# Layer A's input branches of quarters 2 to 4 by seven half-size block products, token-major

## The chip, the cores and the metric

The kernel runs on one core of a Trainium2 chip. The metric is the device time of one execution in microseconds. The page and the trace come from one profiled execution. TensorE is PE in the rows (its weight loads PEld), VectorE is DVE, ScalarE ACT, GpSimd POOL, and SP issues all the DMAs of this kernel in one queue.

## What is computed

A trunk of two layers on 2048 tokens of width 1024, in float32. Layer A is a gated MLP with mixing among the tokens of a chunk of 128; layer B is dilated attention over three groups of heads that share one K/V. The change is in layer A:

```python
def gmlp_layer(x, c, ada_w, ada_b, norm_g, w_in, sgu_g, w_s, b_s, w_out):
    h = rms_norm(x, norm_g) * (1 + scale) + shift        # 2048 x 1024
    u, v, z = jnp.split(h @ w_in, 3, axis=-1)             # three branches, 2048 x 2048 each
    u = jax.nn.gelu(u)
    v = rms_norm(jax.nn.gelu(v), sgu_g)
    mixed = jnp.einsum('gts,bcsge->bctge', jnp.tril(w_s), v) + b_s.T[...]   # 8 groups of 256
    y = u * mixed * jax.nn.silu(z)
    return x + gate * (y @ w_out)
```

## The kernel before

The tokens go through in four quarters of 512 (Q = 0 to 3 in the code, quarters 1 to 4 here), four tiles of 128 each. For each quarter TensorE does layer A (the branches v, u, z, then the output product o), then the projections for layer B (K/V and three q blocks and a z block). The attention of quarter Q-1 (`attend_local`) runs between the matmuls of quarter Q's layer A, and the rest of the attention in the last quarter's projections and in `finish`.

Each float32 product is made of three matmuls (`mm3`): the operands are split into a high part (ScalarE, L242) and a low part (L246; VectorE, with every fourth on GpSimd once `share` is 4), and high x high, high x low and low x high are summed in a bank of PSUM. A matmul has 512 columns. Weights come through SP as raw tiles of 128x512 (six buffers), and stand as split tiles in eight buffers.

In layer A, `dense` makes v by token: a block of 512 outputs for four tiles of tokens is 96 matmuls, and four blocks make the branch. `v_evac` takes gelu and the sum of squares. `dense_f` makes u and z by feature: 256 outputs for 512 tokens, eight calls of 48 matmuls for each. `mix` forms the spatial product by feature (L637, four matmuls of 128 columns, each two passes in the trace) and adds the bias at L639; the results `mt` are multiplied by gelu(u) at L650 and by silu(z) at L662, and split into `yh` and `yl` (L664, L665), which the product o (`dense(yT, a_w_out, ...)`) reads.

In layer B, `dense_s` makes 1024 outputs for 512 tokens by seven products of half the size in each direction instead of eight: seven times 24 matmuls, where the plain form has 192. It reads seven combinations of blocks of the input (`make_ops`: 11, 12, 22, s1 to s4) and combinations of weight blocks that `combine_weights` forms once (four subtractions on GpSimd per step, four steps per block of 1024 columns) and stores in HBM (`wt`). Sums of products are made on VectorE at L361 into tiles `st`. The next product on the same two banks can begin only when they have been emptied.

What runs between matmuls is a list of generators, `fillers`. Each `tick` adds `rate` to a counter, and `fill` takes one step of the next generator for each whole number, in turn. So `rate` sets how thickly attention, the next quarter's input (`make_hA`), the modulation vectors (`ada_acc`) and the weight combinations are spread over the matmuls. `drain` runs the list to its end. The engines' queues are in order; a scheduler that merges the streams decides the order within each, and most buffers are pools whose waits it sets.

The functions that the change touches, and what calls them, with the line numbers of the profile:

## Time and profile before

| what | value |
|---|---|
| median of 3 runs | 3120.85 us (3115.68 to 3136.62) |
| profiled execution | 3119.88 us; its span 3118.1 us |
| mean granted TensorE clock | 0.986 |
| TensorE busy | 2991.9 us, 96% |
| VectorE, ScalarE, GpSimd busy | 1943.9 us, 1629.5 us, 1207.0 us |
| DMA | 547.81 MB, 176 GB/s in the mean |
| layer A of quarter 1: v, u, z, o begin | 28.4, 142.6, 248.6, 355.7 us |
| layer A of quarters 2, 3, 4: v begins | 688.3, 1358.7, 2036.0 us |
| o begins in quarters 2, 3, 4 | 1020.9, 1708.1, 2391.8 us |
| layer B's projections begin in quarters 1 to 4 | 447.5, 1116.6, 1803.7, 2482.6 us |
| last output stage begins | 2834.6 us |

The stages are cut where the first matmul of each begins. A row of the table by stage gives the busy time of each engine in such a stretch. A row of a group gives busy time and the mean duration of one instruction in ns, then the idle time of the engine before it and what ended that. Busy time of TensorE says little by itself, since its matmuls overlap; the distance from start to start is its pace.

### The profile page before, as it was taken

What the parts mean: (1) busy time and instruction counts of PE and PEld (TensorE: products, weight loads), DVE (VectorE), ACT (ScalarE), POOL (GpSimd) and SP (SyncE); (2) the same over time, 40 slices, a digit from 0 to 9 for tenths busy, and PEclk for the clock granted to TensorE, in tenths of its full rate; (3) what the DMA queues carried; (4) which work ended last, traced back from release to release, by engine and by line L of the source; (5) the groups of instructions that cost most, each with busy time, mean ns of one, the idle gap of its engine ahead of it and who ended that gap; (6) DMA issues with size and microseconds to landing.
All of it is one profiled execution on the core that took longest, in us unless ns stands there. A gap on an engine that the chain in (4) does not pass through costs nothing.

```text
span 3118.1 us, 45175 instructions
## 1 busy us (share of the span) xinstructions
PE 2991.9 (96%) x14928; PEld 2500.8 (80%) x14928; DVE 1943.9 (62%) x3286; ACT 1629.5 (52%) x3325; POOL 1207.0 (39%) x1376
## 2 busy tenths in 40 slices
PE   6998999999999999999999999999999999999999
PEld 5887778778888777788887878778888788877787
DVE  6765457673567376765677276756676476767861
ACT  4422335557556245566466265566465357767540
POOL 4134335551124235644245145634344252244332
PEclk9999999999999999999999999999999999999999
DMA  7877647673433367663433366743433356678742
GB/s 232 272 248 250 227 153 222 220 234 120 149 105 105 93 193 232 206 207 115 140 102 98 98 201 205 241 163 106 133 108 102 122 182 210 223 241 283 236 154 95
DMA packets 341182, 547.81 MB, mean 176 GB/s; under 512 B 35818, under 2 KB 135372, under 8 KB 340948
## 3 DMA queue, kind: packets, MB, share of 16 engines
q1 hardware_dynamic: 340948, 544.93, 54.4%
q8 instruction: 118, 1.93, 0.3%
q14 instruction: 116, 0.95, 0.1%
HBM read 439.28 MB, written 105.52 MB: 175 GB/s over the span
## 4 chain that ended last, share of the span: by engine, by line
PE 62%; POOL 8%; DMA 8%; issue 6%; DVE 4%; ACT 3%; SPq 1%; POOLq 0%; DVEq 0%; ACTq 0%
PE pd_o L264 11%; PE pd_v L264 8%; PE pd_kv L264 7%; PE po L969 3%; PE pd_u L301 3%; PE pd_u L299 3%; PE pd_u L300 3%; PE pd_z L299 2%; PE pd_z L301 2%; PE pd_z L300 2%; DMA qt<-qd 1%; PE pm L637 1%; PE pq L857 1%; DMA cw<-in_b_w_in_dram 1%; PE pf L1145 1%
## 5 line engine op out<-in xcount | busy, mean ns | idle before, releaser
L264 PE MATMUL pd_v<-w_v,hAh 128*128 128x512 f32 x1024 | 328.8, 402 | 1.2 <-ACT hAh L425 1.2
L264 PE MATMUL pd_o<-w_o,yh 128*128 128x512 f32 x1024 | 320.9, 394 | 2.1 <-ACT z L660 1.8
L264 PE MATMUL pd_kv<-w_kv,hkh 128*128 128x512 f32 x768 | 245.0, 398 | 3.4 <-DVE w_kv L246 3.2
L264 PEld LDWEIGHTS pd_o<-w_o,yh 128*128 128x128 f32 x1024 | 193.7, 190 | 43.6 <-ACT z L660 2.3
L264 PEld LDWEIGHTS pd_v<-w_v,hAh 128*128 128x128 f32 x1024 | 190.4, 192 | 40.3 <-issue 1.7
L299 PE MATMUL pd_z<-hAh,w_z 128*128 128x512 f32 x512 | 207.6, 405 | 12.8 <-ACT z L660 12.7
L299 PE MATMUL pd_u<-hAh,w_u 128*128 128x512 f32 x512 | 206.4, 403 | 0.0
L908 ACT ACTIVATE pr<-pr,stat,rt 128x256 f32<-128x256 f32 (+1 forms) x320 | 177.4, 556 | 53.4 <-DVE stat L902 31.4
L264 PE MATMUL pd_v<-w_v,hAl 128*128 128x512 f32 x512 | 203.0, 397 | 0.0
L301 PE MATMUL pd_z<-hAh,w_z 128*128 128x512 f32 x512 | 202.3, 395 | 0.0
L300 PE MATMUL pd_z<-hAl,w_z 128*128 128x512 f32 x512 | 201.6, 394 | 0.0
L264 PE MATMUL pd_o<-w_o,yl 128*128 128x512 f32 x512 | 200.8, 392 | 0.0
L301 PE MATMUL pd_u<-hAh,w_u 128*128 128x512 f32 x512 | 200.4, 391 | 0.0
L300 PE MATMUL pd_u<-hAl,w_u 128*128 128x512 f32 x512 | 199.7, 390 | 0.0
L264 PEld LDWEIGHTS pd_kv<-w_kv,hkh 128*128 128x128 f32 x768 | 145.7, 191 | 38.2 <-DVE w_kv L246 7.8
L242 ACT ACTIVATE w_o<-raw_o 128x512 fp32r<-128x512 f32 x128 | 80.0, 629 | 176.4 <-PE pd_o L264 128.7
L242 ACT ACTIVATE w_z<-raw_z 128x512 fp32r<-128x512 f32 x128 | 77.5, 626 | 178.2 <-DMA raw_z<-in_a_w_in_dram 74.9
L242 ACT ACTIVATE w_u<-raw_u 128x512 fp32r<-128x512 f32 x128 | 79.2, 630 | 169.7 <-PE pd_u L301 101.8
L969 PEld LDWEIGHTS po<-kv,pT 128*128 128x128 f32 x1200 | 148.0, 192 | 16.0 <-POOL pT L943 6.6
L969 PE MATMUL po<-kv,pT 128*128 128x128 f32 x1200 | 151.9, 277 | 7.3 <-POOL pT L943 6.2
L264 PE MATMUL pd_kv<-w_kv,hkl 128*128 128x512 f32 x384 | 152.5, 397 | 0.0
L246 DVE TENSOR_TENSOR w_o<-raw_o,w_o 128x512 fp32r<-128x512 f32 x96 | 68.6, 720 | 132.0 <-ACT w_o L242 131.4
(686 smaller groups left out, 7998.4 us busy)
## 6 DMA issues: line engine op xcount, KB each, us to landing
raw_q<-in_b_w_in_dram SPq DMA_DIRECT2D x144, 256.0 KB, 3.5
raw_v<-in_a_w_in_dram SPq DMA_DIRECT2D x128, 256.0 KB, 4.1
raw_u<-in_a_w_in_dram SPq DMA_DIRECT2D x128, 256.0 KB, 2.7
raw_z<-in_a_w_in_dram SPq DMA_DIRECT2D x128, 256.0 KB, 3.1
raw_o<-in_a_w_out_dram SPq DMA_DIRECT2D x128, 256.0 KB, 2.7
qt<-qd SPq DMA_DIRECT2D x96, 260.0 KB, 3.3
raw_kv<-in_w_kv_dram SPq DMA_DIRECT2D x96, 256.0 KB, 3.0
od<-ot SPq DMA_DIRECT2D x96, 256.0 KB, 3.0
```

The lines of the kernel that those rows point to most:

```text
L242: nc.scalar.activation(hi, src, AF.Copy)
L246: e.tensor_tensor(lo, src, hi.bitcast(F32), ALU.subtract)
L264: last_mm[0] = nc.tensor.matmul(pt, a, u[:, w, :], start=f, stop=e, skip_group_check=more)
L299: nc.tensor.matmul(pts[i], wh, hh[:, k, :], start=k == 0, stop=False)
L300: nc.tensor.matmul(pts[i], wh, hl[:, k, :], start=False, stop=False)
L301: nc.tensor.matmul(pts[i], wl, hh[:, k, :], start=False, stop=k == KT - 1)
L637: nc.tensor.matmul(pm[:, t * P:(t + 1) * P], m[e // 8][:, t, (e % 8) * P:(e % 8 + 1) * P], wst[:, e // 2, :], start=True, stop=True)
L857: nc.tensor.transpose(pq[:, h * P:(h + 1) * P], u["qt"][:, h * P:(h + 1) * P], ident)
L908: nc.scalar.activation(pr[:, i, :], pr[:, i, :], AF.Exp, bias=mneg[:, i:i + 1], scale=u["rt"][:, h:h + 1], accum_out=lsum[:, i:i + 1])
L969: nc.tensor.matmul(po[:, h * P:(h + 1) * P], u["pT"][h // hp][:, h % hp, j, :], u["kv"][:, j, kh, 1, :], start=j == 0, stop=j == nk - 1)
L1145: nc.tensor.matmul(pt, yb[:, 0, k, :], wh[:, k, :], start=k == 0, stop=False)
```

## The change

In quarters 2 to 4 the branches v, u and z are made by `dense_s`, two blocks of 1024 outputs each, and all by token. `make_hA` now forms the seven input combinations instead of one pair of high and low parts. `combine_weights` forms the weight combinations of six more blocks, 24 steps more; a step is now loaded, subtracted and stored in three different turns, in buffers of attention that are idle in the first quarter (`rooms`). `layer_A_in` scales v by VectorE between the products of u (`plan`, `jobs`), mixes by token (32 matmuls of 256 columns, L805), gates the result in place with gelu(u) and then silu(z), and turns it to features with 64 transposes per quarter (`to_features`): half of them after the fourth product of z's second block, half at the end. Quarter 1 keeps its form. The rates of the fillers change, and attention is no longer bound to end with z: it runs on into o.

```diff
+    blocks = {f"b{b}": (b_w_in, b * D) for b in range(4)}
+    for j in range(2):
+        blocks.update({f"u{j}": (a_w_in, j * D), f"v{j}": (a_w_in, AW + j * D),
+                       f"z{j}": (a_w_in, 2 * AW + j * D)})
...
     def combine_weights():
...
+        for i in range(len(todo) + 2):
+            if 0 <= i - 2:
+                store(i - 2)
+            yield
+            if i < len(todo):
+                load(i)
+            yield
+            for h in range(2):
+                if 0 <= i - 1 < len(todo):
+                    combine(i - 1, h)
                 yield
...
-    def dense_s(ops, b, nm, evac):
+    def dense_s(ops, b, nm, evac, jobs=()):
+        while b not in combined:
+            fill(1)
...
+            done[0] += 1
+            for n, job in jobs:
+                if n == done[0]:
+                    job()
...
     def layer_A(Q, hA, m, sqv, j0):
+        if Q:
+            return layer_A_out(Q, layer_A_in(Q, hA, m, sqv))
...
+    def layer_A_in(Q, ops, m, sqv):
+        for j in range(2):
+            def ev(t, src, n, j=j):
+                v_evac(Q, m, sqv, 2 * j + n)(t, src[:, 0:512])
+            dense_s(ops, f"v{j}", f"v{Q}{j}", ev)
...
+            for t in ts_:
+                mb = m[j][:, t, n * 512:(n + 1) * 512]
+                nc.vector.scalar_tensor_tensor(mb, mb, rv[:, t:t + 1], gs_[c], ALU.mult, ALU.mult)
...
+        for j in range(2):
+            def ev(t, src, n, j=j):
+                mb = m[j][:, t, n * 512:(n + 1) * 512]
+                pm = pst(f"pm{Q}_{j}{n}{t}")
+                for i in range(2):
+                    gs = slice(i * 256, (i + 1) * 256)
+                    nc.tensor.matmul(pm[:, gs], wst[:, 4 * j + 2 * n + i, :], mb[:, gs],
+                                     start=True, stop=True)
+                u = evt(f"u{Q}_{j}{n}{t}")
+                nc.scalar.activation(u, src[:, 0:512], AF.Gelu_apprx_tanh)
...
+                    nc.vector.scalar_tensor_tensor(mb[:, gs], pm[:, gs], late["bsc"][:, g:g + 1], u[:, gs],
+                                                   ALU.add, ALU.mult)
+            dense_s(ops, f"u{j}", f"u{Q}{j}", ev, plan[j])
...
+            for k in range(KT):
+                py = pst(f"py{Q}_{j}{k}")
+                for t in range(TPQ):
+                    nc.tensor.transpose(py[:, t * P:(t + 1) * P], m[j][:, t, k * P:(k + 1) * P], ident)
+                nc.scalar.activation(yh[:, k, :], py, AF.Copy)
+                nc.vector.tensor_tensor(yl[:, k, :], py, yh[:, k, :].bitcast(F32), ALU.subtract)
+        for j in range(2):
+            def ev(t, src, n, j=j):
+                mb = m[j][:, t, n * 512:(n + 1) * 512]
+                z = evt(f"z{Q}_{j}{n}{t}")
+                nc.scalar.activation(z, src[:, 0:512], AF.Silu)
+                nc.vector.tensor_tensor(mb, mb, z, ALU.mult)
+            dense_s(ops, f"z{j}", f"z{Q}{j}", ev, [(4, lambda: to_features(0))] if j else ())
+        to_features(1)
+        return yT
...
-    fillers.append(side_work())
-    rate[0], share[0] = 1.9, 1 << 20
+    side = combine_weights()
+    fillers.extend([delayed(rest_of_ada()), side])
+    rate[0], share[0] = 2.4, 1 << 20
     for Q in range(NQ):
         if Q > 0:
             fillers.append(attend_local(Q - 1, True))
-            rate[0] = 1.4
+            share[0] = 4
+            rate[0] = 1.2 if Q > 1 else 1.8
```

The new order on three engines is seen at one place each; rows of the changed kernel have its own line numbers (L268 is the matmul of `mm3`, L250 the low part in `split`, L416 a sum in `dense_s`). First TensorE in the third quarter's u branch; `pd_u` is the product's bank, `pm` the mixing. Before:

```order
L299 MATMUL pd_u_1_13478<-hAh_10613,w_u_13536 128x512
L300 MATMUL pd_u_1_13478<-hAl_10614,w_u_13536 128x512
L301 MATMUL pd_u_1_13478<-hAh_10613,w_u_13536 128x512
L637 MATMUL pm_8_13553<-wst,m_1_11865 128x128 x4
L637 MATMUL pm_9_13562<-wst,m_1_11865 128x128 x4
L299 MATMUL pd_u_0_13571<-hAh_10613,w_u_13573 128x512
```

After (`hoa` are the input's combinations, `w_u20t` a combined weight tile, `wst` the mixing weights):

```order
L268 MATMUL pd_u20a_13722<-w_u_3_13911,hoa_11854 128x512 x3
L268 MATMUL pd_u20a_13723<-w_u_3_13911,hoa_11854 128x512 x3
L805 MATMUL pm_000_13954<-m_0_12615,wst 128x256 x2
L805 MATMUL pm_001_13961<-m_0_12615,wst 128x256 x2
L268 MATMUL pd_u20b_13724<-w_u20t_0_13968,hoa_11854 128x512 x3
L268 MATMUL pd_u20b_13725<-w_u20t_0_13968,hoa_11854 128x512 x3
```

The mixing now stands behind the third product of a block, with two matmuls of 256 columns for a tile of tokens, and the next product on the other pair of banks follows it.

Second SP's queue in the first quarter, where the weights of o (`raw_o`) are loaded. Before (`wt` are stores of combined weights, `cw` the tiles that they were formed in, `xr` the residual's tiles):

```order
L326 DMA wt_0_115<-cw_2811 128x512
L253 DMA raw_o_0_3_2888<-in_a_w_out_dram 128x512
L326 DMA wt_1_116<-cw_2813 128x512
L326 DMA wt_2_117<-cw_2811 128x512
L326 DMA wt_3_118<-cw_2813 128x512
L253 DMA raw_o_0_4_2893<-in_a_w_out_dram 128x512
L673 DMA xr_2_2856<-in_x_dram 128x1024
L673 DMA xr_3_2858<-in_x_dram 128x1024
L253 DMA raw_o_0_5_2898<-in_a_w_out_dram 128x512
```

After (the letters b, v, u in `cw` and `wt` tell the block):

```order
L257 DMA raw_o_1_4_3122<-in_a_w_out_dram 128x512
L343 DMA cwkTv_2_3169<-in_a_w_in_dram 128x1024
L343 DMA cwqTv_2_3170<-in_a_w_in_dram 128x1024
L359 DMA wtv_0_123<-cwprv_10_3071 128x512
L359 DMA wtv_1_124<-cwpTv_11_3074 128x512
L359 DMA wtv_2_125<-cwprv_11_3072 128x512
L359 DMA wtv_3_126<-cwpTv_10_3073 128x512
L257 DMA raw_o_1_5_3127<-in_a_w_out_dram 128x512
L359 DMA wtv_0_123<-cwkTv_2_3169 128x512
L359 DMA wtv_1_124<-cwqTv_2_3170 128x512
L359 DMA wtv_2_125<-cwkTv_2_3169 128x512
L359 DMA wtv_3_126<-cwqTv_2_3170 128x512
```

Before, three of the combining's sixteen steps had their stores from here on; now the combining of v and u goes on among o's weights through the whole stage.

Third VectorE in the third quarter's z branch. Before (`w_z` is the low part of a weight tile, `pT` and `pr` belong to attention):

```order
L246 TENSOR_TENSOR w_z_14748<-raw_z_14749,w_z_14748 128x512
L965 TENSOR_TENSOR stat_176<-stat_176,stat_177 128x4
L246 TENSOR_TENSOR w_z_14765<-raw_z_14766,w_z_14765 128x512
L246 TENSOR_TENSOR w_z_14799<-raw_z_14800,w_z_14799 128x512
L940 TENSOR_TENSOR pT_6_00_14568<-pp_6_0_14563,upto 128x2x128
L942 TENSOR_TENSOR pT_6_00_14568<-pp_6_0_14563,pT_6_00_14568 128x2x128
L940 TENSOR_TENSOR pT_6_01_14572<-pp_6_0_14563,upto 128x2x128
L942 TENSOR_TENSOR pT_6_01_14572<-pp_6_0_14563,pT_6_01_14572 128x2x128
L662 TENSOR_TENSOR mt_0_12955<-mt_0_12955,z_6_14582 128x512
L662 TENSOR_TENSOR mt_0_12955<-mt_0_12955,z_7_14587 128x512
```

After (`st_z21u` are sums of products, `w_z21t` low parts of combined weight tiles):

```order
L250 TENSOR_TENSOR w_z_0_15546<-raw_z_0_15547,w_z_0_15546 128x512
L250 TENSOR_TENSOR w_z_1_15551<-raw_z_1_15552,w_z_1_15551 128x512
L1095 TENSOR_TENSOR stat_201<-stat_200,stat_201 128x4
L416 TENSOR_TENSOR st_z21u_15461<-pd_z21a_15376,st_z21u_15461 128x512
L1020 TENSOR_TENSOR kT_6_15498<-pk_6_15493,kT_6_15498 128x512
L1030 SCALAR_TENSOR_TENSOR qT_6_0_15506<-pq_6_0_15501,gqk,qT_6_0_15506 128x512
L416 TENSOR_TENSOR st_z21u_15462<-pd_z21a_15377,st_z21u_15462 128x512
L1140 TENSOR_TENSOR ot_5_0_15541<-po_5_0_15532,st_o_0_15347 128x512
L250 TENSOR_TENSOR w_z_2_15556<-raw_z_2_15557,w_z_2_15556 128x512
L250 TENSOR_TENSOR w_z21t_0_15613<-raw_z21t_0_15614,w_z21t_0_15613 128x512
L250 TENSOR_TENSOR w_z21t_1_15618<-raw_z21t_1_15619,w_z21t_1_15618 128x512
L250 TENSOR_TENSOR w_z21t_2_15623<-raw_z21t_2_15624,w_z21t_2_15623 128x512
```

Low parts of weights follow each other more closely, and sums that empty the banks stand between them and the attention's operations.

171 lines of the change are left out of this document (133 added, 38 removed).

## The prediction

> **What bounds the kernel now.** I read the busy line of the page first, then the busy times by stage, then the spacing of single instructions on the engine that turned out to be full. In the table of stages the columns are the stretch, its length, then for PE, PEld, DVE, ACT and POOL the busy time and the number of instructions, then the granted clock, the DMA share and GB/s.
>
> ```profile
> PE 2991.9 (96%) x14928; PEld 2500.8 (80%) x14928; DVE 1943.9 (62%) x3286; ACT 1629.5 (52%) x3325; POOL 1207.0 (39%) x1376
> ...
> 28.40:142.60 114.20, 107.76 (x470) 86.94 (x471) 83.45 (x127) 49.88 (x100) 28.39 (x26) 0.94 0.71 233
> 142.60:248.60 106.00, 106.00 (x554) 90.74 (x552) 73.47 (x108) 29.14 (x52) 31.30 (x24) 1.00 0.78 252
> 248.60:355.70 107.10, 92.47 (x386) 73.75 (x385) 50.10 (x55) 33.29 (x58) 51.47 (x36) 0.94 0.78 255
> 355.70:447.50 91.80, 91.54 (x401) 74.88 (x402) 39.68 (x63) 32.28 (x62) 14.52 (x13) 0.98 0.46 147
> 447.50:643.70 196.20, 187.27 (x817) 152.99 (x816) 137.03 (x190) 110.01 (x209) 114.93 (x144) 0.98 0.68 219
> 643.70:688.30 44.60, 42.23 (x193) 33.70 (x192) 37.59 (x49) 25.69 (x46) 31.01 (x35) 1.00 0.75 247
> ...
> 1316.60:1358.70 42.10, 41.17 (x191) 33.41 (x189) 35.49 (x46) 24.76 (x44) 28.80 (x31) 1.00 0.79 264
> 1358.70:1471.30 112.60, 111.36 (x586) 94.33 (x585) 58.18 (x117) 71.34 (x148) 41.33 (x54) 1.00 0.39 127
> 1471.30:1594.40 123.10, 123.10 (x698) 106.84 (x696) 78.07 (x145) 59.56 (x110) 44.30 (x54) 1.00 0.40 127
> 1594.40:1708.10 113.70, 111.94 (x594) 95.22 (x594) 80.66 (x159) 78.88 (x142) 56.26 (x64) 1.00 0.36 110
> 1708.10:1803.70 95.60, 92.50 (x417) 76.92 (x416) 38.24 (x56) 28.30 (x55) 21.75 (x18) 0.98 0.37 111
> ...
> 1994.60:2036.00 41.40, 40.80 (x190) 33.38 (x189) 29.39 (x44) 22.71 (x42) 25.92 (x29) 1.00 0.77 260
> ```
>
> The first six rows are v, u, z, o, most of the B projections and the z block of the first quarter. The rows from 1358.70 to 1803.70 are v, u, z and o of the third quarter, 445.0 us together, and stand for the quarters that are changed. TensorE is busy in 98 to 100% of the three branches there, while VectorE stands at 52 to 71% and the DMA engines at 36 to 40%. So in these branches an instruction that TensorE no longer issues is time saved, as long as the others can follow. In the first quarter it is not only TensorE: in its z stage TensorE is busy for 92.47 of 107.10 us with the DMA engines at 0.78.
>
> Busy time is not pace, since matmuls overlap in the records, so the pace is read from starts.
>
> ```profile
> 1852.51 5.44 PE pd_q22a L264 x24
> ...
> 1483.13 0.28 PE L893 MATMUL ps<-kT,qT 128*128 128x256 f32 x1
> ...
> 1484.57 0.39 PE L299 MATMUL pd_u<-hAh,w_u 128*128 128x512 f32 x1
> ...
> 1485.96 1.95 PE L637 MATMUL pm<-wst,m 128*128 128x128 f32 x16
> 1487.66 0.48 PE L299 MATMUL pd_u<-hAh,w_u 128*128 128x512 f32 x1
> ...
> 1490.48 0.60 PE L857 MATMUL pq<-ident,qt 128*128 128x128 f32 x4
> 1490.83 0.48 PE L299 MATMUL pd_u<-hAh,w_u 128*128 128x512 f32 x1
> 1491.15 0.39 PE L300 MATMUL pd_u<-hAl,w_u 128*128 128x512 f32 x1
> ```
>
> One half-size product of 24 matmuls takes 5.44 us, which is 0.2267 us for each 512-wide matmul. Twelve 256-wide ones stand between 1483.13 and 1484.57, 0.12 us each. Sixteen mixing passes take from 1485.96 to 1487.66, 1.70 us. Four transposes take 0.35 us, and the matmul behind them needs 0.32 instead of 0.23 us, so 0.44 us for a group of four.
>
> **The products.** Each of the three branches covers 2048 outputs in two blocks of 1024. A block costs 7 products x 24 = 168 matmuls where it cost 192, so a quarter goes from 1152 to 1008: 144 x 0.2267 = 32.6 us less, and 98 us less in three quarters.
>
> **The transposes.** The gated result now stands by token and is turned with 64 transposes per quarter, 16 groups of four: 16 x 0.44 = 7.0 us, 21 us in three quarters. The input transposes stay at 32 per quarter.
>
> **The mixing.** Before, eight groups of sixteen passes, with the same 0.08 us at the switch: 8 x 1.78 = 14.2 us per quarter. Now 32 matmuls of 256 columns, 64 passes. No pass of that kind stands in the trace; the nearest is the 256-wide attention product at 0.12 us, which gives 7.7 us and some 1.3 us of switches. Between no gain (a wide pass costs two narrow ones) and 7 us of gain I take 5 us per quarter, 15 in all. TensorE's own work falls by 98 - 21 + 15 = 92 us. All of this was TensorE's time in stages where TensorE was the last to be waited for, so 92 us is the gain if nothing else gets late.
>
> **What gets late: VectorE.** Prices of one instruction are in the next rows (busy time, mean ns).
>
> ```profile
> L246 DVE TENSOR_TENSOR w_u<-raw_u,w_u 128x512 fp32r<-128x512 f32 x104 | 78.1, 759 | 66.9 <-ACT w_u L242 66.7
> L246 DVE TENSOR_TENSOR w_kv<-raw_kv,w_kv 128x512 fp32r<-128x512 f32 x72 | 70.2, 1007 | 8.8 <-ACT w_kv L242 8.3
> L361 DVE TENSOR_TENSOR st_q30u<-pd_q30a,st_q30u 128x512 f32<-128x512 f32 x2 | 1.4, 684 | 0.0
> L587 DVE SCALAR_TENSOR_TENSOR acc_a<-aw,sc,acc_a 128x512 f32<-128x512 f32 x28 | 33.6, 1201 | 1.0
> L630 DVE TENSOR_SCALAR m<-m,rv 128x1024 f32<-128x1024 f32 x32 | 26.5, 861 | 13.3 <-POOL rv L234 13.3
> L639 DVE SCALAR_TENSOR_TENSOR mt<-pm,colsb,b_s 128x512 f32<-128x512 f32 x64 | 47.1, 744 | 28.9 <-PE pm L637 28.7
> L650 DVE TENSOR_TENSOR mt<-mt,u 128x512 f32<-128x512 f32 x64 | 56.5, 896 | 16.9 <-ACT u L649 13.8
> L665 DVE TENSOR_TENSOR yl<-mt,yh 128x512 fp32r<-128x512 f32 x40 | 43.8, 1127 | 4.7 <-ACT yh L664 2.8 <-PE pd_z L300 1.6
> L898 DVE SCALAR_TENSOR_TENSOR pr<-dist,rt,ps 128x256 f32<-128x256 f32 (+1 forms) x320 | 122.5, 430 | 37.1 <-PE ps L895 24.6 <-PE ps L889 12.2
> L1108 DVE TENSOR_TENSOR yb<-pyb,yb 128x512 fp32r<-128x512 f32 x32 | 20.9, 685 | 8.3 <-ACT yb L1107 8.3
> L246 POOL TENSOR_TENSOR w_u<-raw_u,w_u 128x512 fp32r<-128x512 f32 x24 | 32.3, 1344 | 109.0 <-ACT w_u L242 108.9
> ```
>
> Per changed quarter: a block splits 28 weight tiles instead of 16, so 72 more, of which VectorE takes three in four, 54 x 0.759 = 41.0 us. Ten sums a block, 60 x 0.684 = 41.0. The scaling of v is 16 operations of a kind that lies between 0.685 (yb) and 1.201 (acc_a); at 0.95 it is 15.2, in place of 8 x 0.861 = 6.9. The mixing's output is taken in 32 operations of 256 elements, 32 x 0.430 = 13.8, in place of 16 x (0.744 + 0.896) = 26.2. The low part of y costs 16 x 0.685 = 11.0 in place of 8 x 1.127 = 9.0. The sum is 122.0 - 42.1 = 79.9 us more. VectorE did 58.18 + 78.07 + 80.66 + 38.24 = 255 us in 445 and would do 335 in 445 - 31 = 414, that is 81% instead of 57%. It isn't even: by the order, v, u, z and o of the third quarter hold 133, 172, 188 and 107 of VectorE's instructions, so u and z, a bit over 100 us each, ask for some 96 and 105 us. VectorE is nearly full there, and it stands ahead of TensorE twice: it makes the weights' low parts, and it empties the banks that the product after next writes.
>
> The trace shows both answers to a full VectorE, the first two rows here, with DMA at its fullest as well in the first. (Columns as above.)
>
> ```profile
> 160.00:180.00 20.00, 20.00 (x102) 16.98 (x102) 19.13 (x31) 4.88 (x8) 0.00 (x0) 1.00 0.95 317
> 440.00:460.00 20.00, 17.37 (x77) 13.79 (x75) 18.58 (x26) 12.19 (x25) 13.10 (x11) 0.91 0.64 221
> 280.00:300.00 20.00, 12.66 (x55) 9.82 (x53) 7.79 (x9) 4.43 (x8) 7.39 (x6) 0.87 0.78 244
> ```
>
> At 160 us VectorE is 96% busy, GpSimd rests, and TensorE loses nothing. At 440 us VectorE is 93% busy, GpSimd 65%, and TensorE loses 13%. Block products under 71 to 84% of VectorE are the three z blocks of the first table: 168 x 0.2267 + 8 x 0.44 = 41.6 us of work took 44.6, 42.1 and 41.4 us, a loss of 7, 1 and 0%. So the loss of the 228.5 us of products per quarter (1008 x 0.2267) lies between 0 and 13%, 0 to 30 us. The branches' load lies above that of the z blocks and below that of 440 us, and I take 5% more than now: 11 us per quarter, 33 us in all. ScalarE gains 72 splits but stays behind: it was busy for 71 of 113 us in its fullest stage.
>
> A rule of the Trainium skill speaks against this change here ("SBUF — State Buffer", section "Who interferes with whom"): a VectorE instruction with two inputs in SBUF and a GpSimd instruction that reads SBUF exclude each other, and the later one waits for the whole of the earlier. The rows agree with it: the same subtraction takes 759 ns in one branch and 1007 where GpSimd is busier. The sum above goes by the row's 759; what the rule would make of it is the third case below.
>
> **The first quarter.** The added blocks' sums are made here and at the start of the second quarter: 24 more steps of 1 MB read and 1 MB written. By the order the o stage issues 29.1 MB where it issued 10.2, and the B projections 70.1 where it was 55.2. So 355.7 to 688.3 us must carry 99 MB instead of 65, 298 GB/s, against the 147, 219 and 247 of their rows. The row at 160 us shows 317 GB/s with TensorE full, so it can be borne, with little to spare. GpSimd's part, 96 subtractions, has cover: it works 14.52 of 91.80 us in the o stage. On the other side the stores now stand two steps behind their subtractions in SP's queue, so the weights behind them no longer wait for GpSimd; the row at 280 us, TensorE busy for 12.66 of 20 us, is of that kind, and with its neighbours some 20 us could come back. Between -20 us and the loss in the fourth case I take +10 us, nearer to what the row at 160 us shows.
>
> **The sum.** The profiled execution took 3119.9 us (a span of 3118.1), which is 1 us under the median of 3120.85. 3119.9 - 98 + 21 - 15 + 33 + 10 = 3071 us.
>
> **The cases.** First, the forecast: 3071 us, between 3045 and 3095 with the stall between 1 and 8%. Chance 0.50.
>
> Second, all the new work is covered: no stall beyond today's and 20 us back in the first quarter, 3071 - 33 - 30 = 3008 us. For it speaks the row at 160 us, against it the rows at 440 and 643.70 us. Chance 0.15.
>
> Third, VectorE becomes the bound in u and z: with GpSimd busy for 164 of 445 us, a two-input operation of VectorE meets one of GpSimd in about four of ten cases and waits for half of its 1.34 us. That is 0.27 us on each of some 120 such operations per quarter, 32 us, of which the row's 759 ns over an undisturbed 685 holds 9. If two thirds of the rest reach TensorE, the stall grows by 15 us per quarter: 3117 us. By the row of 440 us, 13% or 30 us per quarter in place of 11, it is 3071 + 57 = 3128 us. No measurable change. Chance 0.20. The page named above states the mechanism; the numbers are those of the rows.
>
> Fourth, slower: the one DMA queue doesn't go beyond the 255 GB/s of the z stage while it mixes 512 KB reads and stores with the weights. Then 99 MB take 389 us where 332.6 were, and the 100 MB before them 394 us where 355.7 were: +94 us in place of +10, 3155 us. It decides from about 270 GB/s downwards. Against it speaks the row at 160 us, for it that no stretch of the first table goes above 264. Chance 0.15.
>
> **Range and chances.** What a measurement of this kernel can tell from no change is about 1%, 31 us: faster means below 3090, slower above 3152. Faster holds the second case and nine tenths of the first, 0.60. Within 1% holds the rest of the first and most of the third, 0.22. Slower holds the fourth and the tail of the third, 0.18. The range from 3010 to 3140 reaches over the second and third cases and leaves out the fourth; the likeliest case alone has 3045 to 3095.
>
> **What would show it.** The v, u and z stages of the third quarter should take some 310 us together in place of 349.4, with o longer than 95.6 (attention now runs on into it), 425 us for all four. The 512-wide matmuls of the branches should be 3024 in quarters 2 to 4 where they were 3456. VectorE should stand at 80% over the four, over 90% in u and z. If the product rows show a spacing well above 0.24 us and the wait lines name VectorE's splits or sums, the third case holds; if the first quarter ends after 720 us with TensorE waiting for loads, the fourth. A first quarter that ends before 680 us speaks for the second. I would be wrong as a whole if the B projections, whose work does not change, slowed down.

## The result: no gain, half a per cent slower

The changed kernel took 3139.72 us (median of 11 runs, 3132.84 to 3145.52), the kernel before beside it 3121.43 us (11 runs, 3115.68 to 3136.62). The ratio is 1.0056, 95% interval 1.0042 to 1.0071: within the 1% that I called no change, on the slow side of it, and 69 us above the forecast of 3071, at the very end of the range. The profiled execution took 3141.98 us, a span of 3140.3.

The busy line of its page, then the table of stages (columns as in the prediction): v, u, z, o, B projections and z block of the first quarter; v, u, z, o of the third and its z block; the fourth quarter; the finish.

```profile
PE 2939.4 (94%) x14496; PEld 2441.4 (78%) x14496; DVE 2247.5 (72%) x3727; ACT 1754.9 (56%) x3594; POOL 1357.9 (43%) x1451
```

```profile
28.10:140.80 112.70, 104.37 (x454) 82.36 (x454) 74.18 (x102) 45.85 (x94) 49.21 (x41) 0.97 0.68 225
140.80:250.40 109.60, 107.00 (x552) 90.54 (x553) 89.56 (x120) 32.28 (x57) 36.48 (x26) 1.00 0.87 294
250.40:339.50 89.10, 89.10 (x404) 74.00 (x403) 70.17 (x75) 38.06 (x65) 44.54 (x28) 1.00 0.96 334
339.50:444.80 105.30, 94.04 (x401) 77.17 (x400) 62.57 (x65) 27.84 (x53) 63.15 (x45) 0.94 0.85 292
444.80:670.90 226.10, 195.62 (x810) 157.75 (x809) 152.44 (x218) 112.93 (x211) 120.67 (x153) 0.94 0.77 260
670.90:712.40 41.50, 41.50 (x201) 34.77 (x200) 34.71 (x48) 28.62 (x51) 17.61 (x20) 1.00 0.74 249
...
1379.50:1484.50 105.00, 100.28 (x513) 84.13 (x512) 73.81 (x133) 80.47 (x162) 45.19 (x52) 0.97 0.58 184
1484.50:1600.60 116.10, 110.34 (x549) 92.59 (x548) 96.78 (x175) 69.23 (x128) 43.47 (x44) 0.99 0.57 179
1600.60:1708.50 107.90, 103.25 (x559) 87.18 (x557) 98.11 (x186) 79.93 (x151) 55.28 (x59) 1.00 0.56 179
1708.50:1817.10 108.60, 105.85 (x531) 89.04 (x530) 63.97 (x112) 42.19 (x91) 36.67 (x39) 0.98 0.38 121
2012.00:2056.50 44.50, 41.36 (x178) 33.30 (x178) 34.06 (x44) 29.14 (x53) 29.56 (x31) 0.96 0.81 271
2056.50:2853.80 797.30, 749.47 (x3937) 629.65 (x3935) 575.29 (x1095) 512.02 (x1112) 316.82 (x367) 0.98 0.58 186
2853.80:3140.30 286.50, 271.30 (x1552) 231.53 (x1552) 182.66 (x337) 119.70 (x334) 88.90 (x56) 0.98 0.54 182
```

Three things are to be seen. First, the branches of the third quarter: v, u and z take 329.0 us where they took 349.4, and o 108.6 where it was 95.6, so the four together fall from 445.0 to 437.6 only; over the three quarters by stage starts it is 19.6 us. TensorE, 98 to 100% busy there before, is at 95 to 96%, and VectorE at 83% in u and 91% in z. Second, the first quarter ends at 712.4 and not at 688.3: its z stage fell from 107.1 to 89.1 us, its o rose from 91.8 to 105.3, its B projections from 240.8 to 267.6. Third, TensorE loses 11 of 105 us in that o and 30 of 226 in those B projections, with the granted clock at 0.94.

The longest waits of TensorE from o to the end of the first quarter name VectorE (who waited for what, us in total, times, longest); what VectorE itself waited for is taken up with the runs:

```profile
PE pt_b L502 <- DVE xr L860: 11.1, 2, 8.0
PE pd_kv L268 <- DVE w_kv L250: 8.7, 2, 6.3
PE pd_q00b L268 <- DVE st_q00u L416: 4.8, 1, 4.8
```

Split by stage starts, the 22 us between the two profiled executions are: 19.6 gained in layer A of quarters 2 to 4, 24 lost in the first quarter, 18 lost in the B projections and the finish after it (0.2, 7.1 and 7.5 in the three quarters, 2.9 in the finish).

### The profile page after: what moved, and what is told of

It is laid out like the page before. It is cut to its first block, busy times and chain, and to the rows that moved or that the text cites. A ratio compares the mean times of both kernels' runs of the same rounds, so it can differ in the third digit from the quotient of the medians.

```text
span 3140.3 us, 46154 instructions
## 1 busy us (share of the span) xinstructions
PE 2939.4 (94%) x14496; PEld 2441.4 (78%) x14496; DVE 2247.5 (72%) x3727; ACT 1754.9 (56%) x3594; POOL 1357.9 (43%) x1451
## 5 line engine op out<-in xcount | busy, mean ns | idle before, releaser
L268 PE MATMUL pd_o<-w_o,yh 128*128 128x512 f32 x1024 | 325.6, 397 | 3.3 <-DVE w_o L250 3.3
L268 PE MATMUL pd_kv<-w_kv,hkh 128*128 128x512 f32 x768 | 246.9, 401 | 11.1 <-DVE w_kv L250 10.2
L268 PEld LDWEIGHTS pd_o<-w_o,yh 128*128 128x128 f32 x1024 | 192.0, 190 | 41.6 <-DVE w_o L250 3.7
L268 PE MATMUL pd_o<-w_o,yl 128*128 128x512 f32 x512 | 202.3, 395 | 0.0
L268 PEld LDWEIGHTS pd_kv<-w_kv,hkh 128*128 128x128 f32 x768 | 146.2, 192 | 46.3 <-DVE w_kv L250 14.9
L1136 PEld LDWEIGHTS po<-kv,pT 128*128 128x128 f32 x1200 | 147.2, 192 | 12.5 <-ACT pT L986 4.0
L268 PE MATMUL pd_kv<-w_kv,hkl 128*128 128x512 f32 x384 | 152.3, 397 | 0.0
L250 DVE TENSOR_TENSOR w_o<-raw_o,w_o 128x512 fp32r<-128x512 f32 x104 | 89.9, 875 | 77.5 <-ACT w_o L246 74.9
L1065 DVE SCALAR_TENSOR_TENSOR pr<-dist,rt,ps 128x256 f32<-128x256 f32 (+1 forms) x320 | 122.4, 429 | 19.5 <-PE ps L1062 13.7
L246 ACT ACTIVATE w_q<-raw_q 128x512 fp32r<-128x512 f32 x144 | 87.6, 626 | 77.6 <-DMA raw_q<-in_b_w_in_dram 49.6
L1083 POOL TENSOR_TENSOR dg<-pr,ident 128x256 f32<-128x256 f32 x76 | 63.3, 833 | 155.8 <-ACT pr L1075 130.1
L1110 POOL TENSOR_TENSOR pT<-pT,dg 128x256 f32<-128x256 f32 x76 | 64.9, 855 | 113.9 <-DVE pT L1109 105.5
L268 PEld LDWEIGHTS pd_o<-w_o,yl 128*128 128x128 f32 x512 | 97.4, 190 | 20.4
L250 DVE TENSOR_TENSOR w_q<-raw_q,w_q 128x512 fp32r<-128x512 f32 x117 | 88.4, 779 | 33.5 <-ACT w_q L246 33.3
L1034 DVE COPY rt<-qt 128x8 f32<-128x8 f32 x96 | 26.0, 273 | 116.2 <-DMA qt<-qd 116.2
L1312 PE MATMUL pf<-wo,yb 128*128 128x512 f32 x256 | 105.6, 413 | 2.6 <-ACT yb L1274 2.6
L246 ACT ACTIVATE w_kv<-raw_kv 128x512 fp32r<-128x512 f32 x96 | 57.0, 630 | 84.3 <-PE pd_o L268 49.6
L1313 PE MATMUL pf<-wo,yb 128*128 128x512 f32 x256 | 101.9, 398 | 0.0
```

The source lines that it names most:

```text
L246: nc.scalar.activation(hi, src, AF.Copy)
L250: e.tensor_tensor(lo, src, hi.bitcast(F32), ALU.subtract)
L268: last_mm[0] = nc.tensor.matmul(pt, a, u[:, w, :], start=f, stop=e, skip_group_check=more)
L1034: nc.vector.tensor_copy(rt[:, 0:8], u["qt"][:, 512:520])
L1065: nc.vector.scalar_tensor_tensor(pr[:, i, :], dist[:, 256 - w:256], u["rt"][:, h:h + 1], psc[:, i, :], ALU.mult, ALU.add)
L1083: nc.gpsimd.tensor_tensor(dg, prev, ident.unsqueeze(1).broadcast_to([P, hp, P]), ALU.mult)
```

## The experiments

The time of a run is its median; the ratio is to the kernel before on the same chip, with its 95% interval.

**What the combining costs.** Two edits: the combining alone, and everything but the combining.

```diff
 # comb_only: layer_A and make_hA as before, ten blocks combined
-        if Q:
-            return layer_A_out(Q, layer_A_in(Q, hA, m, sqv))
```

> The three input branches of all quarters as in the kernel before, with the combining of all ten blocks as in the changed kernel; the sums of the six new blocks are stored and not read, so the output is the old one. Theory (the first quarter's loss is the price of combining six more blocks; it is 24 us by the two traces): Q2's first v product starts at about 712 us and not at 688, and the whole takes about 3121 + 24 = 3145 us, 3138 to 3155. Rival (the combining is hidden, and the first quarter lost its time because the changed order of other fillers, or one noisy execution): 3115 to 3130 us.

3149.57 us, 1.0095 (1.0062 to 1.0128). The second quarter began at 708.6 us in place of 688.3, and from there to the end it was within 5 us of the kernel before. So the combining, with the other layer A untouched, makes the kernel slower by about what the first quarter loses (the medians lie 28 us apart), and the theory holds.

```diff
 # no_comb
-        todo = [(b, k) for b in ("b2", "b1", "b0", "b3", "v0", "v1", "u0", "u1", "z0", "z1")
+        todo = [(b, k) for b in ("b2", "b1", "b0", "b3")
...
-            rate[0] = 1.2 if Q > 1 else 1.8
+            rate[0] = 1.2
...
-                rate[0] = 1.2 if Q else 1.4
+                rate[0] = 1.2
```

The products read plain quarter blocks in place of the stored sums, and the side work of the first two quarters is released at a lower pace.

> The changed kernel, but the six blocks of layer A are not combined: their products read four plain quarter blocks of a_w_in in place of the stored sums, so instructions and loads of the products stay as many while 24 steps of 1 MB read and 1 MB written and 96 subtractions are gone. The numbers that come out are not the reference's. Theory (the combining costs what o and B of the first quarter got longer, 13.5 + 26.8 us, while the 18 us that z of the first quarter got shorter come from the stores' place two steps behind their subtractions): the second quarter starts at about 670 us and the whole takes about 3140 - 42 = 3098 us, 3088 to 3108. Rival (the first quarter's low parts, all on VectorE up to the end of its B projections, cost the time): within 10 us of 3140.

3057.44 us, 0.9799 (0.9784 to 0.9813): 82 us less, twice what was expected. The second quarter began at 665.1. But 13.6 us came in the second quarter, which had held the last of the combining's steps, and 26 in the fourth and the finish, where nothing had been taken away. Both are taken up below.

```diff
 # comb_nosub
             t1, t3, t4, t2 = quads[i]
+            if todo[i][0][0] != "b":
+                return
```

> The changed kernel, but the 96 subtractions of the six new blocks are left out; their loads and stores of 1 MB each stay, so the products read plain quarter blocks from the stored copies and the numbers are not the reference's. Leaving out loads, stores and subtractions took the first quarter from 712 to 665 us and the second from 667 to 653. Theory (the subtractions on GpSimd lengthen VectorE's low parts, 1172 ns each in the o stage, and those hold TensorE): most of it goes here too, the second quarter starts at 675 to 685 us, the whole takes 3080 to 3105 us. Rival (the 48 MB of traffic delay the weights' loads): the second quarter starts at 700 to 712 us and the whole takes 3120 to 3140 us.

3097.66 us, 0.9918 (0.9895 to 0.9941). The second quarter began at 668.1, not at 712.4: the subtractions, not the traffic, were 44 of the first quarter's price, and the traffic 3. In the trace of the changed kernel 76 of the 96 stand in the first quarter, 41 in o and 35 in the B projections; the other 20 cost nothing, since the second quarter takes 667.2 us without them and 667.1 with them. The o stage here, at 342 GB/s and 0.97 of the DMA engines, left TensorE all but full; the next line is the B projections:

```profile
338.80:429.20 90.40, 89.05 (x402) 73.65 (x401) 39.64 (x65) 27.27 (x53) 2.02 (x4) 1.00 0.97 342
429.20:626.50 197.30, 184.53 (x809) 150.94 (x808) 136.43 (x217) 112.10 (x212) 69.58 (x113) 0.99 0.86 295
```

What 63 us of GpSimd do to VectorE stands in its groups of the o stage (mean ns of one ahead of the second bar). The changed kernel first, then the one without the subtractions:

```profile
L250 DVE TENSOR_TENSOR w_o<-raw_o,w_o 128x512 fp32r<-128x512 f32 x25 | 29.1, 1172 | 20.5 <-ACT w_o L246 18.0 <-DMA cwkTu<-in_a_w_in_dram 1.0 <-DMA cwprv<-in_a_w_in_dram 0.7
L770 DVE TENSOR_TENSOR yl<-mt,yh 128x512 fp32r<-128x512 f32 x8 | 10.4, 1364 | 1.1 <-PE pd_z L304 1.1
L853 DVE TENSOR_TENSOR xr<-xr,xo 128x512 f32<-128x512 f32 x6 | 6.9, 1192 | 0.0
L852 DVE TENSOR_TENSOR xo<-pd_o,ga 128x512 f32<-128x512 f32 x6 | 4.0, 686 | 12.8 <-PE pd_o L268 12.8
```

```profile
L250 DVE TENSOR_TENSOR w_o<-raw_o,w_o 128x512 fp32r<-128x512 f32 x25 | 17.3, 692 | 30.3 <-ACT w_o L246 29.5 <-DMA cwpTv<-in_a_w_in_dram 0.7
L772 DVE TENSOR_TENSOR yl<-mt,yh 128x512 fp32r<-128x512 f32 x8 | 5.0, 686 | 1.1 <-PE pd_z L304 1.1
L854 DVE TENSOR_TENSOR xo<-pd_o,ga 128x512 f32<-128x512 f32 x6 | 4.0, 688 | 17.2 <-PE pd_o L268 17.2
L855 DVE TENSOR_TENSOR xr<-xr,xo 128x512 f32<-128x512 f32 x6 | 3.9, 684 | 0.0
```

Three kinds with both inputs in SBUF go from 692, 686 and 684 ns to 1172, 1364 and 1192. The fourth has the same shape, but one input in PSUM (pd_o): 688 and 686. The rule of the Trainium skill that the prediction weighed ("SBUF — State Buffer", section "Who interferes with whom") says just this: two SBUF inputs meet GpSimd's reads, one does not. The rows agree.

But the longest wait of TensorE in the changed kernel's o stage is not a wait for a stretched split. In these rows of its timeline (start, length, engine, line, what) the brackets hold the idle time of the engine before the row and what ended it:

```profile
429.02 1.26 POOL L349 TENSOR_TENSOR cwkTu<-cwkTu 128x512 f32<-128x512 f32 x1 [3.50 <-DMA cwkTu<-in_a_w_in_dram]
...
435.04 0.55 POOL L238 TENSOR_TENSOR r_b<-r_b,mhalf 128x1 f32<-128x1 f32 x1
...
435.62 0.75 DVE L860 TENSOR_SCALAR xr<-xr,r_b 128x1024 f32<-128x1024 f32 x1 [6.94 <-POOL r_b L238]
...
436.52 1.09 PE L502 MATMUL pt_b<-ident,xr 128*128 128x128 f32 x4 [8.00 <-DVE xr L860]
```

A subtraction of the combining waited 3.5 us for its load at the head of GpSimd's queue. The small operation `r_b`, a factor of the normalisation, stood behind it and three more subtractions, though its input was ready at 427.0 us. VectorE stood idle for `r_b`, and TensorE for the tile that VectorE scales by it. The wait of 6.3 us for `w_kv` (486.2 us) and those of 4.2 us for `hs_k` (517 to 520 us) go back to the same thing: GpSimd waited 5.5 and 6.2 us for a load of the combining, and VectorE 7.2 and 5.8 us for what stood behind. That is 18.5 of the 42 us that TensorE waits from o to the end of the quarter; without the subtractions it waits 14 us in all.

```diff
 # comb_dve: four lines of this kind
-                nc.gpsimd.tensor_tensor(t1, t3, t1, ALU.subtract)
+                nc.vector.tensor_tensor(t1, t3, t1, ALU.subtract)
```

> The changed kernel, but all 160 subtractions of the combining (the ten blocks) run on VectorE and none on GpSimd. Theory (a GpSimd operation on SBUF locks VectorE out for its whole 1.3 us, so that 96 of them cost the first quarter 44 us; on VectorE the same work costs its own 0.69 us each, 160 x 0.69 = 110 us spread over 570 us of which VectorE has 67% busy): the first quarter ends at 680 to 695 us in place of 712, the whole takes about 3113 us, 3100 to 3127. Rival (VectorE is the engine that is short, so that more work on it costs more): 3135 to 3165 us.

3120.29 us, 0.9993 (0.9980 to 1.0005), and the second quarter began at 696.7. VectorE, the engine that seemed short, took on 160 more operations and the kernel became 19 us faster than the changed one. The rival falls; the gain is 7 us smaller than the theory's, and the second quarter starts 2 us later than its bound. So of the 44 us that the subtractions cost the first quarter, 16 go when they leave GpSimd, and 28 stay. A part of these is the same wait at the same place, now in VectorE's own queue:

```profile
421.69 0.69 DVE L349 TENSOR_TENSOR cwkTu<-cwkTu 128x512 f32<-128x512 f32 x1 [5.12 <-DMA cwkTu<-in_a_w_in_dram]
...
428.15 1.09 PE L502 MATMUL pt_b<-ident,xr 128*128 128x128 f32 x4 [6.89 <-DVE xr L860]
```

How the 28 us divide between such waits and VectorE's own time for the subtractions was not separated.

```diff
 # late_comb: old layer A in quarter 2, where the six blocks are combined
-        if Q:
+        if Q > 1:
...
-            rate[0] = 1.2 if Q > 1 else 1.8
+            rate[0] = 1.2 if Q > 1 else 2.7
+            if Q == 1:
+                fillers.append(combine_weights(("v0", "v1", "u0", "u1", "z0", "z1"), False))
```

> The first two quarters keep the old layer A, quarters 3 and 4 have the seven products; the first quarter combines the four blocks of b_w_in in the new order, and the six blocks are combined during layer A of the second quarter, where the DMA engines were 36 to 40% busy and GpSimd some 40%. Theory (combining is cheap where the engines have room: 8 of 24 steps cost 6 us at the start of the second quarter where the rest cost 45 in the first): 3100 for the new order, + 18 for 24 steps, - 16 for two quarters of layer A, + 8 for the longer preparation of the input: about 3110 us, 3095 to 3122. Rival (24 steps cost some 45 us wherever they stand): 3130 to 3150 us.

3171.08 us, 1.0156 (1.0127 to 1.0186): both expectations were too low. v, u and z of the second quarter took 116.4, 137.5 and 121.6 us where the same stages took 102.3, 115.5 and 111.7 in b4_order (below), without combining and at a pace of 1.4, and the steps that were left over were flushed in the first B projection. The u stage, then that projection:

```profile
773.30:910.80 137.50, 119.63 (x624) 101.32 (x623) 68.71 (x116) 58.41 (x118) 49.66 (x40) 0.94 0.64 208
...
1130.80:1228.90 98.10, 54.18 (x212) 41.06 (x211) 48.21 (x61) 26.53 (x54) 56.22 (x45) 0.77 0.68 226
```

These 98.1 us were 53.5 in b4_order. That part is the pace I gave it, not the place. In the u stage GpSimd is 36% busy and VectorE 50%, and TensorE still loses 18 us of 137.5. Of these, 12.5 are one wait for attention's tiles, behind this row of VectorE:

```profile
882.27 0.17 DVE L1068 COPY rt<-qt 128x8 f32<-128x8 f32 x1 [21.54 <-DMA qt<-qd]
```

VectorE stood idle for 21.5 us until a load of attention arrived, which SP had issued at 879.5 us, right behind a store of the combining. Room on an engine's busy line was no room for this work.

**The four blocks in the new order.**

```diff
 # b4_order, against the kernel before: old layer A, four blocks, new combine_weights
...
+            if i < len(todo):
+                load(i)
...
+                if 0 <= i - 1 < len(todo):
+                    combine(i - 1, h)
```

> The kernel before with one part of the change alone: the four blocks of b_w_in are combined in the new order, with their stores two steps behind the subtractions and with the borrowed tiles; layer A is the old one in all quarters and its six blocks are not combined. Theory (the 18 us that the first quarter's z stage got shorter come from this order, and nothing takes them back): the first quarter ends at about 667 us in place of 688 and the whole takes about 3121 - 21 = 3100 us, 3092 to 3108. Rival (the time is lost again at the next wait): 3113 to 3125 us.

3086.65 us, 0.9884 (0.9861 to 0.9908), better than expected: the first quarter ends at 656.8, 31.5 us earlier than before. Its z, o, and B projections with z block:

```profile
251.70:340.70 89.00, 89.00 (x403) 73.94 (x402) 66.98 (x74) 37.61 (x65) 44.47 (x28) 1.00 0.97 333
340.70:429.70 89.00, 89.00 (x402) 73.68 (x402) 39.64 (x65) 27.39 (x53) 2.40 (x4) 1.00 0.38 119
429.70:615.20 185.50, 183.49 (x821) 151.17 (x820) 139.78 (x218) 112.13 (x213) 70.18 (x114) 1.00 0.65 209
615.20:656.80 41.60, 41.08 (x189) 33.33 (x188) 35.51 (x56) 25.47 (x45) 16.92 (x23) 1.00 0.82 271
```

z and o are TensorE's own time. But the order of the stores doesn't come alone: with it come the borrowed buffers, another pace of the side work, and splits that stay on VectorE up to the end of the first quarter, where the kernel before gives every fourth to GpSimd from o on. By stages 18.1 us are gained in z, 2.9 in o and 13.6 in the B projections and their z block, and 3.1 lost in v and u. Against the kernel without combining, whose first quarter is the same up to the preparation of the next input and ends at 665.1, it also prices that preparation, which makes the operands' sums and runs at a slightly higher pace: 8.3 us.

**What paces the branches.**

```diff
 # no_low, in the branches of quarters 2 to 4
         nc.scalar.activation(hi, src, AF.Copy)
+        if not low:
+            return
```

> The changed kernel, but in the three branches of quarters 2 to 4 the weights' low parts are not computed, and the matmul that used them uses the high part a second time: TensorE and the loads have the same work, VectorE loses 126 of 168 subtractions a quarter and GpSimd 42. This leaves out a part of the computation. Theory (VectorE's load paces the branches): VectorE falls from 74% to some 50% in v, u, z and o, lower than in the kernel before (57%), the stall of TensorE falls from some 37 us per quarter to some 12, and the whole takes 3140 - 75 = 3065 us, 3050 to 3085. Rival (TensorE waits for banks, for the order of the sums or for transposes, whatever VectorE's load): 3120 to 3140 us.

3076.12 us, 0.9861 (0.9846 to 0.9876): 64 us less. v, u, z and o of the third quarter:

```profile
1360.60:1459.20 98.60, 97.11 (x513) 82.59 (x512) 45.22 (x96) 80.80 (x165) 24.59 (x38) 1.00 0.61 194
1459.20:1566.50 107.30, 107.30 (x550) 91.65 (x548) 60.41 (x129) 67.54 (x124) 18.79 (x28) 1.00 0.63 196
1566.50:1669.60 103.10, 102.09 (x559) 87.36 (x557) 67.11 (x147) 78.26 (x146) 32.76 (x46) 1.00 0.58 185
1669.60:1775.10 105.50, 104.36 (x531) 87.82 (x529) 62.34 (x112) 43.16 (x94) 36.38 (x39) 1.00 0.39 123
```

414.5 us in place of 437.6 with as many matmuls and loads. So the low parts, three in four of them on VectorE, pace the branches. They seldom do it directly: of the 17.5 us that TensorE waits in the changed kernel's four stages, 4.5 name a split, and the others mostly attention's tiles, which are made in the same queues; here it waits 3.6 us. The other 31 us that separate 414.5 from the old 445.0 are what the products were to bring.

The next two move the same work between the engines, one way and the other:

```diff
-            share[0] = 4
+            share[0] = 2          # share2, layer A of quarters 2 to 4
+            share[0] = 1 << 20    # all_dve, the same place
```

> The changed kernel, but in layer A of quarters 2 to 4 every second low part of a weight is computed on GpSimd and not every fourth: VectorE gives up 42 x 0.82 = 34 us per quarter, GpSimd gets 42 x 1.34 = 56 us more. Theory (VectorE's own load is what counts): the stall of 37 us per quarter falls by about a third, 3140 - 30 = 3110 us, 3100 to 3125. Rival (the two engines get in each other's way, so that the work only moves): 3135 to 3165 us, with VectorE's subtractions of the weights longer than now (0.75 to 0.91 us each).

3134.71 us, 1.0049 (1.0032 to 1.0066): 5 us, the rival's case. In v, u, z and o of the third quarter VectorE's busy time fell by 21 us and not by 34 (311.81 in the sum line of its stage table; the four rows of the changed kernel add up to 332.67), since what it kept got longer: a v split takes 1115 ns here and 908 in the changed kernel (its row follows under the next run).

```profile
sum 433.50, PE 417.42 PEld 352.92 DVE 311.81 ACT 271.26 POOL 248.72; mean PE 104.35 PEld 88.23 DVE 77.95 ACT 67.81 POOL 62.18
```

```profile
L250 DVE TENSOR_TENSOR w_v<-raw_v,w_v 128x512 fp32r<-128x512 f32 x10 | 11.1, 1115 | 2.0 <-ACT w_v L246 1.8
```

> The changed kernel, but in layer A of quarters 2 to 4 all low parts of the weights are computed on VectorE, none on GpSimd (one in four before): 42 more per quarter on VectorE, 56 us less on GpSimd. Theory (VectorE's own load counts): leaving out 126 a quarter on VectorE gave 63 us in three quarters, 0.17 us for each, so 126 more in three quarters cost about 21 us, more where VectorE is already at 91%: 3155 to 3190 us. Rival (the two engines exclude each other, so that GpSimd's 1.34 us cost VectorE as much as the work itself): no loss or a gain, 3120 to 3145 us, with VectorE's subtractions of the weights shorter than 0.75 to 0.91 us.

3118.59 us, 0.9987 (0.9975 to 0.9999): 21 us faster with more work on the engine that is short, the rival's case again. The v splits of the branches in the changed kernel, with a share of four, and then here:

```profile
L250 DVE TENSOR_TENSOR w_v<-raw_v,w_v 128x512 fp32r<-128x512 f32 x15 | 13.2, 908 | 1.5 <-ACT w_v L246 1.5
```

```profile
L250 DVE TENSOR_TENSOR w_v<-raw_v,w_v 128x512 fp32r<-128x512 f32 x24 | 16.2, 708 | 2.0 <-ACT w_v L246 1.8
```

24 splits cost VectorE 16.2 us where 15 cost 13.2. So a good part of what a split cost VectorE was its neighbour's work. By stage starts, layer A of the three quarters took 1300.2 us in the changed kernel, 1281.4 here and 1234.7 without low parts: GpSimd's share of the splits cost 19 us, the splits themselves 47.

**Both edits, and the old layer A with them.** comb_all_dve joins the edits of comb_dve and all_dve. every_dve also takes GpSimd's splits of the B projections, and b4_all_dve is b4_order with all splits on VectorE in quarters 2 to 4; both change the share wherever it is set to four:

```diff
-            share[0] = 4
+            share[0] = 1 << 20
```

> Both edits together: the combining's subtractions on VectorE, and all low parts of layer A's weights in quarters 2 to 4 on VectorE, which alone gave 21 us. Theory (exclusion in both places, in different quarters, so that the gains add): about 3113 - 21 = 3092 us, 3078 to 3106. Rival (VectorE is short in one of them): 3118 to 3150 us.

3113.97 us, 0.9968 (0.9951 to 0.9985), between the two: 6 us beyond comb_dve, so the gains of 19 and 21 us do not add. Its first quarter ended at 701.1 where comb_dve's ended at 696.7 with the same instructions up to there; why the rest is missing stays open. The profiled first quarters say how much one of them can: no_low, share2, phase and all_dve have the changed kernel's instructions up to there, and end at 712.5, 709.4, 709.0 and 703.9 us, the changed kernel at 712.4. A difference of less than 9 us between two first quarters with the added subtractions is no finding. By the means of these five and of the three with the subtractions on VectorE (695.1 in the next run) the 16 us above are 12.

> The changed kernel with the combining's subtractions and all low parts of the weights on VectorE, in the B projections too. Without the last it took 3114 us; in the old layer A the step to all low parts on VectorE gave 30 us, in o and the B projections. Theory (GpSimd's operations hold up VectorE wherever it is near full): 3114 - 20 = 3094 us, 3082 to 3104, and so still behind the old layer A with both edits (3057 us). Rival (with the longer preparation of the input VectorE is itself short in the B projections): 3107 to 3130 us.

3089.39 us, 0.9894 (0.9876 to 0.9913), as the theory had it.

> The old layer A with the four blocks combined in the new order (3087 us), but with all low parts of the weights on VectorE in quarters 2 to 4, in layer A and in the B projections. Theory (GpSimd's low parts cost wherever VectorE is near full, which is in the B projections, 70 to 84% busy): some 10 us less, 3070 to 3083 us. Rival (in a kernel where TensorE is 98% busy nothing waits for it): 3083 to 3093 us, or up to 3105 if VectorE becomes short in the B projections.

3056.55 us, 0.9777 (0.9759 to 0.9795): the fastest kernel that leaves nothing out, 65 us below the median of before and 83 below the changed one, and 30 below b4_order where 10 were expected. Theory and rival are each right in a part of the stages: v, u and z of the second quarter take 102.3, 115.5 and 111.7 us in b4_order and 102.3, 115.4 and 111.7 here, since TensorE is full there. The gain is mostly in o and the B projections. In the third quarter's o TensorE no longer waits 4.9 us for a tile of attention that GpSimd makes. Two lines of b4_order, u of the second quarter and o of the third, then the same o stage here and the busy line:

```profile
759.10:874.60 115.50, 115.50 (x634) 99.16 (x633) 60.83 (x107) 62.56 (x120) 14.87 (x15) 1.00 0.41 128
...
1673.20:1770.90 97.70, 92.84 (x418) 77.06 (x417) 39.13 (x56) 28.44 (x55) 21.12 (x18) 0.97 0.37 114
```

```profile
1667.00:1757.70 90.70, 90.70 (x417) 75.42 (x416) 42.95 (x64) 27.69 (x54) 10.13 (x9) 1.00 0.40 123
```

```profile
PE 2963.5 (97%) x14928; PEld 2484.0 (81%) x14928; DVE 2012.2 (66%) x3526; ACT 1623.6 (53%) x3321; POOL 871.3 (29%) x1136
```

Against it every_dve, with the splits placed alike and the changed layer A, loses 37 us in the first quarter (695.1 to 658.2) and gains 7 in all that follows: 29 in layer A of the three quarters, less 22 lost in the B projections and the finish.

**The 26 us without a cause.** Two more kernels without combining, and the changed one with the side work released at other moments.

```diff
 # no_comb2: the quarter blocks in the stored copies' order
-            (w_, 4 * (i // 2), n0 + 512 * (i % 2))
+            (w_, 4 * (i % 2), n0 + 512 * (i in (1, 2)))
```

> As the kernel without combining (3057 us), but the plain quarter blocks stand in the order in which the kernel without the subtractions (3098 us) reads its stored copies, so that the two compute the same wrong numbers and differ in 24 loads and stores of 1 MB alone. In the profile of the first the fourth quarter and the finish were 26 us shorter than in any kernel with the same instructions there. Theory A (those 26 us hang on the numbers, through the clock that TensorE is granted, which was 1.00 in its finish and 0.98 in the others): the fourth quarter comes back to its 1084 us and the whole takes 3075 to 3090 us. Theory B (they come from the stored blocks, which other kernels read from another place): 3050 to 3062 us.

3052.80 us, 0.9769 (0.9754 to 0.9783). The numbers are not the cause; theory A falls, and what B says is only that it lies in the program.

```diff
 # no_comb_rates
-            rate[0] = 1.2
+            rate[0] = 1.2 if Q > 1 else 1.8
...
-                rate[0] = 1.2
+                rate[0] = 1.2 if Q else 1.4
```

> The kernel without combining and with the plain quarter blocks in the stored copies' order (3053 us), but with side work released at the pace of the changed kernel in the first two quarters (1.8 and 1.4 per step where it had 1.2). Against the kernel that loads and stores without subtractions (3098 us) it lacks the 24 loads and stores of 1 MB alone. Theory (pace and interleaving make the 45 us): 3075 to 3100 us, with the second quarter's v stage near 102 us in place of 89. Rival (the traffic makes them): 3046 to 3062 us, v near 89 us.

3082.87 us, 0.9867 (0.9844 to 0.9890). With the pace of the slower kernel 30 of the 45 us are back, with the same numbers, the same blocks and none of the traffic. In the profiled executions it is 21, and 17 of them lie in the fourth quarter and the finish, where the pace is the same in both and only the interleaving has shifted. The last 15 us, to 3097.66, are those of the traffic in the second quarter, which takes 653.3 us here, 653.1 in no_comb2 and 667.2 with the loads and stores; the first quarter ends at 667.2 here and at 668.1 with them.

```diff
 # phase
+            if Q == 3:
+                rate[1] = 0.5
```

> The changed kernel, with the counter that releases the side work (attention) set half a step ahead at the start of the fourth quarter: the same instructions in another interleaving there and nothing else. Theory (the interleaving alone moves the last quarter and the finish by amounts like the 26 us that came without a change of work): those 1084 us change by 8 to 26 us, in either direction, and the whole leaves 3132 to 3147. Rival (the interleaving is worth little, and the 26 us have another cause): within 5 us there, the whole 3133 to 3146 us.

3128.02 us, 1.0014 (1.0002 to 1.0026), 12 us less than the changed kernel. The fourth quarter and the finish of its profiled run:

```profile
2052.80:2837.60 784.80, 744.53 (x3938) 625.53 (x3936) 576.50 (x1096) 508.95 (x1110) 319.65 (x367) 0.99 0.60 189
2837.60:3118.30 280.70, 269.29 (x1552) 229.27 (x1552) 177.04 (x337) 119.15 (x334) 89.16 (x56) 1.00 0.56 186
```

1065.5 us in place of 1083.8, for the same instructions half a step apart. This execution is the fastest of its ten, 8 us under their median, so not all of the 18 us is interleaving; by the medians it is worth 12. So the 10 us that the fourth quarter's B projections and the finish lost against before cannot be put down to the change's work, and 12 of the 18 us that separate the two medians hang on it.

## Why the prediction was wrong, step by step

Forecast and measurement against the profiled time of before (3119.9), in us. The sum missed by 71 us: 28 in the stalls of the branches, 18 in the B projections and the finish, 14 in the first quarter and 11 in the mixing.

| term | forecast | by the runs | from |
|---|---|---|---|
| products | -98 | -98 | 432 fewer in the busy line, x 0.2267 as in the forecast |
| transposes | +21 | +21 | 48 groups x 0.44; four take 0.35 and the matmul behind them 0.32 in its trace too |
| mixing | -15 | -4 | starts, below |
| stalls in the branches | +33 | +61 | the rest of the -19.6 in layer A |
| first quarter | +10 | +24 | its end |
| B projections 2 to 4, finish | 0 | +18 | stage starts |
| sum | -49 | +22 | |

**The products** were right, and so was the bound: without the weights' low parts the third quarter's four stages take 414.5 us, some 31 less than before.

**The mixing was mis-sized.** The row that I took for a wide pass was not of its kind. In the timeline of the changed kernel (start, length, engine, line, count), a group of the mixing in u of the third quarter starts at 1510.70 and the matmul behind it at 1512.24:

```profile
1510.70 1.89 PE L805 MATMUL pm<-m,wst 128*128 128x256 f32 x8
1512.24 1.73 PE L268 MATMUL pd_u20b<-w_u20t,hoa 128*128 128x512 f32 x6
...
1518.37 0.28 PE L1060 MATMUL ps<-kT,qT 128*128 128x256 f32 x1
1518.49 0.28 PE L1061 MATMUL ps<-kT,qT 128*128 128x256 f32 x1
```

Eight passes of 256 columns take 1.54 us, 0.19 each, where sixteen of 128 took 1.70. The attention products next to them have the same shape in the row and 0.12 us: their operands are fp32r tiles and those of the mixing plain fp32, which the shape column does not tell. No run changes the format alone, so that it makes the difference is not shown. So 8 x (1.54 + 0.08) = 13.0 us a quarter in place of 14.2. The lower end of my bounds, that a wide pass costs two narrow ones, was nearly the truth.

**The stalls were mis-sized**, 61 for 33, and this is the largest error. I priced VectorE's load with a mean of 759 ns, asked what its busy share allowed, and took 5% of the products' 685 us, where the runs gave 9%. The load was the right thing to look at: the low parts cost layer A 47 us even with all of them on VectorE. What the 5% lacked was GpSimd: with its share of the splits moved to VectorE, VectorE did more and layer A took 19 us less; with more of them on GpSimd, it took no less. The third case had this as a surcharge in u and z, and with a chance of 0.20. Its time, 3117 to 3128 us, was the nearest of the four. And some 14 us are the loads and stores of the combining's last steps in the second quarter, which the sum had put into the first. These amounts overlap, so they don't add up to 61.

**In the first quarter two terms were wrong, and one wait.** Measured by the ends of that quarter, from run to run: the new order and what comes with it -31.5 (I said -20), the longer preparation of the input +8.3 (I costed it at nothing), the traffic +3, the subtractions +44.3. As steps of one path they add up to 24 in any case. The step that failed is "GpSimd's part, 96 subtractions, has cover: it works 14.52 of 91.80 us in the o stage". An idle GpSimd is no cover, for two reasons that the traces show. Its work stretches VectorE's operations with two inputs in SBUF, the splits among them, which went from 692 to 1172 ns. And a subtraction that waits for its load at the head of a queue holds back the small results behind it, for which VectorE and then TensorE wait: 18.5 of TensorE's 42 us. Moving the subtractions to VectorE took away the first, left the second in VectorE's own queue, and gave back 12 to 16 of the 44 us. The fourth case looked for the loss in the rate of the DMA queue. It was wrong: the queue carried 342 GB/s with TensorE all but full, not 255.

**The B projections** were to stay as they are, and I wrote that I would be wrong as a whole if they slowed. In the first quarter they did, for the reason above. Of the 18 us later, 7 lie in the third quarter, where the longer preparation of the input runs beside them. These hold in every run: the B projections of that quarter take 238 to 243 us in all kernels with the changed layer A there, and 231 to 236 in those with the old one. For the fourth quarter's and the finish it is 632 to 647 us with the changed layer A and 634 to 636 with the old one and the same share of splits, so what is lost there is within what interleaving moves.

**The other signs.** v, u and z of the third quarter: 310 expected, 329.0 measured; the four stages 425 and 437.6; VectorE 80% and 76%, over 90% in z alone. For the third case I had named wait lines with VectorE's splits or sums: in the three branches TensorE's waits name splits with 4.5 us and sums with none. The first quarter ended before 720, so the fourth case's sign rightly stayed out.
